# A hybrid mLSTM/GLA layer: the modulation sums beside the GLA branch get GpSimd's queue, more accumulators and more gate buffers

## The chip, the cores and the metric

The kernel runs on one core of one Trainium2 chip. Its engines work in parallel, each through its own instructions in order: PE (matmuls), DVE (VectorE), ACT (ScalarE), POOL (GpSimd) and SP (SyncE, which here only issues DMAs). An instruction that waits holds up everything behind it on its engine. DMAs are issued by SP, ACT or GpSimd, each with a queue of its own, and are carried out by 16 DMA engines. The metric is device time in microseconds of one execution; lower is better. The profiled execution is one among these, and times inside the program are counted from its start.

## What is computed

One layer over 1024 latent tokens with 1024 channels, and 256 context tokens. What matters here, cut from the reference:

```python
mod = jax.nn.silu(c) @ w_mod[l] + b_mod[l]                 # 6 x 1024 values, from a 1024 x 6144 matrix
sh1, sc1, g1, sh2, sc2, g2 = jnp.split(mod[:, None, :], 6, axis=-1)
# ... input projections of h * (1 + sc1) + sh1, two mLSTM scans, two GLA scans ...
y_m = (head_norm(h_m, mlstm_norm_g, True) * jax.nn.sigmoid(o_m)) @ w_branch_mlstm
y_g = (head_norm(h_g, gla_norm_g, False) * jax.nn.silu(z_g)) @ w_branch_gla
mix = (jax.nn.sigmoid(gate_a) * y_m + jax.nn.sigmoid(gate_b) * y_g) @ w_out
h = layer_norm(ALPHA * h + g1 * mix, ln1_g[l], ln1_b[l])
f = conv_glu(h * (1 + sc2) + sh2, rows, *ffn)
h = layer_norm(ALPHA * h + g2 * f, ln2_g[l], ln2_b[l])
```

`sh1` and `sc1` are needed at the start. The other 4096 values of `mod` (`g1`, `sh2`, `sc2`, `g2`) are needed only after the branch stages, and are computed in the middle of the kernel: for this 16.8 MB of `w_mod` have to be read.

## The kernel before

Everything is float32. A matmul is made of three in a faster format: each operand is split into a high part (ACT copies it, `L252`) and a low part (DVE or GpSimd subtracts, `L253`), and `mm3` (`L283` to `L285`) adds high x high, high x low and low x high over eight blocks of 128 channels: 24 matmuls of 128 x 512 for one half of an output tile (512 tokens). `wload` loads a weight matrix 256 columns at a time, in four pieces through four `raw` buffers (`L263`, issued by SP), and splits each into `whi` and `wlo` (six buffers each).

The program runs in stages: modulation and projections, the scans with projections beside them, then four stages which this change touches:

- `gated` for the GLA branch: the projection `z_g` is computed, ACT and DVE make the gated value (`L933` to `L939`), which is split into `hi` (ACT) and `lo` (GpSimd), one tile of 128 channels after the other.
- the GLA branch: eight tiles of 128 output channels, two halves each. For a half, a saved `gate_b` half is loaded into `th` (a tile named `gt`, two buffers; SP, `L954`), ACT takes its tanh (`L955`), PE computes `w_branch_gla` times the gated values into PSUM (tags `pj`, `pa`, `po` in turn, two buffers each), DVE multiplies (`L958`), and SP stores the half to DRAM (`ya`, `L959`).
- `gated` for the mLSTM branch, and the mLSTM branch, built the same way (`th` again, `L994` to `L999`).

Beside tile j of the GLA branch the j-th of eight sums of the modulation is made. `mod_sum(j)` takes an accumulator (`acc`, in slot `u17` or `u19` in turn), GpSimd clears it (`L901`), SP loads 512 values of `b_mod` into its first row (`L903`), and four tiles of `w_mod` of 128 x 2 x 512, 512 KB each, come through two buffers in the slots `u16` and `u18` (`L906`, SP). DVE adds each tile with two instructions (`L908`), each multiplying by a column of silu(c). `mod_row(j)` adds the accumulator's 128 partitions with a matmul by ones on PE (`L913`, two matmuls in the profile), DVE copies the result back (`L914`), SP writes it to `md_d` in DRAM (`L915`). Row j - 1 follows tile j. All these slots are also used by the `gated` stages for other data.

The order in which each engine carries out its instructions is fixed when the program is built, by a scheduler that moves instructions ahead where it expects room. So SP's queue mixes loads of weights, of `w_mod`, of gate halves and stores of results, and one that waits holds up the rest. A tile's buffer is used again only when all that read or wrote it has ended; loading from DRAM into it has to wait for that.

Of the kernel before, what the change touches and what calls it, by code (L numbers as in the profile page):

```python
# [6 lines left out]
F32 = mybir.dt.float32  # L7
# [4 lines left out]
ALU = mybir.AluOpType  # L12
# [3 lines left out]
P = 128  # L16
# [20 lines left out]
def layer_kernel(ctx, tc, I, out, dbg=None):  # L37
    nc = tc.nc
    V, A, G, T, SY = nc.vector, nc.scalar, nc.gpsimd, nc.tensor, nc.sync
    I = {n: (a[0] if n not in ("x", "c", "ctx", "c_ctx") else a) for n, a in I.items()}  # L40
# [13 lines left out]
    def nm(s):  # L54
        cnt[0] += 1
        return f"{s}_{cnt[0]}"

    def pt(tag, shape):
        return ps.tile(shape, F32, tag=tag, name=nm(tag))
# [4 lines left out]
    def slot(i, shape, dt=F32):  # L64

        if i in (8, 9, 10, 11) and sl is sl0:
            n = 1
            for w in shape[1:]:
                n *= w
            tag = "kk" if i < 10 else "qq"  # L70
            if i % 2 == 0:
                half[tag] = sl.tile([P, 2, n], dt, tag=tag, name=nm(tag))
            v = half[tag][0:shape[0], i % 2, :]
            return v if len(shape) == 2 else v.rearrange("p (a b) -> p a b", b=shape[2])
        return sl.tile(shape, dt, tag=f"s{i}", name=nm(f"s{i}"))

    def ubt(i, shape, dt=F32):
        return ub.tile(shape, dt, tag=f"u{i}", name=nm(f"u{i}"))

    def drt(name, shape, dt=F32):  # L80
        return dr.tile(shape, dt, tag=name, name=name)
# [6 lines left out]
    scn = ExitStack()  # L88
    sc = scn.enter_context(tc.tile_pool(name="scn", bufs=1))
# [3 lines left out]
    ones = cst.tile([P, 1], F32, name="ones")  # L93
# [59 lines left out]
    sC = cst.tile([P, KD, 2], F32, name="sC")  # L153
# [19 lines left out]
    raw = slot(7, [P, KD, 64])  # L173
# [20 lines left out]
    for k in range(KD):  # L194
        for b in range(3):
            T.matmul(mps[b][0:2, :], sC[:, k, :], wm[2 * k + b // 2][:, b % 2 * 512:b % 2 * 512 + 512],
                     start=k == 0, stop=k == KD - 1)
# [30 lines left out]
    def cB(i):  # L228
        return colB[:, i:i + 1]
# [21 lines left out]
    def split(hi, lo, src, eng=G):  # L251
        A.activation(hi, src, AF.Copy)  # L252
        eng.tensor_tensor(lo, src, hi.bitcast(F32), op=ALU.subtract)  # L253
# [25 lines left out]
    def mm3(p, lhs, rhs, nk=KD):  # L279
        for k in range(nk):  # L280
            lh, ll = lhs(k)
            rh, rl = rhs(k)
            T.matmul(p, lh, rh, start=k == 0, stop=False)  # L283
            T.matmul(p, lh, rl, start=False, stop=False)  # L284
            T.matmul(p, ll, rh, start=False, stop=k == nk - 1)  # L285
# [37 lines left out]
    def proj(w, c, b, tag="pj"):  # L323
        p = pt(tag, [P, 512])
        mm3(p[:, 0:BW[b]], lambda k: w(k, c, P), u_blk(b))
        return p
# [68 lines left out]
    p = proj(w0, P, 2)  # L395
# [144 lines left out]
    def gla_qk(h):  # L540
        w = wload([(w_in, O_QG + h * P, P, 0), (w_in, O_KG + h * P, P, P)], eng=V)
        q = slot(0, [P, SEQ])
        k = slot(1, [P, L])
        for b in range(2):
            p = proj(w, 0, b)
            A.activation(q[:, b * 512:b * 512 + 512], p[:], AF.Identity, scale=QS, bias=cB(c_qg + h))
        for b in range(3):
            p = proj(w, P, b)
            A.activation(k[:, b * 512:b * 512 + BW[b]], p[:, 0:BW[b]], AF.Identity, bias=cB(c_kg + h))
        return q, k  # L550
# [311 lines left out]
    for h in range(GH):  # L862
        q, k = gla_qk(h) if h else (q0, k0)
# [24 lines left out]


    md_d = drt("md_d", [4096])  # L890

    tags = ("pj", "pa", "po")
    seq = [0]

    def ytag():
        seq[0] += 1
        return tags[seq[0] % 3]

    def mod_sum(b):
        acc = ubt((17, 19)[b % 2], [P, 512])  # L900
        G.memset(acc[:], 0.0)  # L901
        c0 = 2048 + b * 512
        SY.dma_start(acc[0:1, :], I["b_mod"][c0:c0 + 512].unsqueeze(0))  # L903
        for k2 in range(0, KD, 2):
            raw = ubt((16, 18)[k2 // 2 % 2], [P, 2, 512])
            SY.dma_start(raw[:], I["w_mod"][k2 * P:(k2 + 2) * P, c0:c0 + 512].rearrange("(k p) c -> p k c", p=P))  # L906
            for i in range(2):
                V.scalar_tensor_tensor(acc[:], raw[:, i, :], sC[:, k2 + i, 0:1], acc[:], op0=ALU.mult, op1=ALU.add)  # L908
        return acc

    def mod_row(b, acc):
        p = pt("pt", [P, 512])
        T.matmul(p[0:1, :], ones[:], acc[:], start=True, stop=True)  # L913
        V.tensor_copy(acc[0:1, :], p[0:1, :])  # L914
        SY.dma_start(md_d[b * 512:b * 512 + 512].unsqueeze(0), acc[0:1, :])  # L915

    def gated(off, cb0, src_d, silu):
        hi, lo = [], []
        for j2 in range(4):
            w = wload([(w_in, off + j2 * 256, 256, 0)])  # L920
            for e in range(2):
                j = 2 * j2 + e
                hi.append(slot(j, [P, SEQ], F32R))
                lo.append(slot(8 + j, [P, SEQ], F32R))
                hr = ubt(16 + j % 2, [P, SEQ])
                SY.dma_start(hr[:], src_d[j][:])
                ht = ubt(18, [P, SEQ])
                zz2 = ubt(19, [P, 2, 512]) if silu else None
                for b in range(2):
                    s_ = slice(b * 512, b * 512 + 512)  # L930
                    p = proj(w, e * P, b, ytag())
                    th = sc.tile([P, 512], F32, tag="gt", name=nm("gt"), bufs=2)
                    A.activation(th[:], p[:], AF.Tanh, scale=0.5, bias=cB(cb0 + j))  # L933
                    hs = hr[:, s_]
                    if silu:
                        zt = zz2[:, b, :]
                        A.activation(zt, p[:], AF.Identity, scale=0.5, bias=cB(cb0 + j))
                        V.tensor_tensor(hs, zt, hs, op=ALU.mult)
                    V.scalar_tensor_tensor(ht[:, s_], th[:], 1.0, hs, op0=ALU.add, op1=ALU.mult)  # L939
                    split(hi[j][:, s_], lo[j][:, s_], ht[:, s_])  # L940
        return hi, lo
# [3 lines left out]
    accs = {}  # L945
    for j2 in range(4):
        w = wload([(I["w_branch_gla"], j2 * 256, 256, 0)])
        for e in range(2):
            j = 2 * j2 + e
            accs[j] = mod_sum(j)  # L950
            for b in range(2):
                s_ = slice(b * 512, b * 512 + 512)
                th = sc.tile([P, 512], F32, tag="gt", name=nm("gt"), bufs=2)
                SY.dma_start(th[:], thb_d[j][:, s_])  # L954
                A.activation(th[:], th[:], AF.Tanh)  # L955
                p = pt(ytag(), [P, 512])
                mm3(p[:], lambda k: w(k, e * P, P), lambda k: (ghi_[k][:, s_], glo_[k][:, s_]))
                V.scalar_tensor_tensor(th[:], th[:], 1.0, p[:], op0=ALU.add, op1=ALU.mult)  # L958
                SY.dma_start(ya_d[j][:, s_], th[:])  # L959
            if j:  # L960
                mod_row(j - 1, accs[j - 1])
    mod_row(7, accs[7])

    rowF = ubt(19, [P, 3, P])
# [19 lines left out]
    for j2 in range(4):  # L984
        w = wload([(I["w_branch_mlstm"], j2 * 256, 256, 0)])
        for e in range(2):
            j = 2 * j2 + e
            ya = ubt(16 + j % 2, [P, SEQ])
            SY.dma_start(ya[:], ya_d[j][:])
            xhi.append(ubt(j, [P, SEQ], F32R))  # L990
            xlo.append(ubt(8 + j, [P, SEQ], F32R))
            for b in range(2):
                s_ = slice(b * 512, b * 512 + 512)
                th = sc.tile([P, 512], F32, tag="gt", name=nm("gt"), bufs=2)  # L994
                SY.dma_start(th[:], tha_d[j][:, s_])
                A.activation(th[:], th[:], AF.Tanh)
                p = pt(ytag(), [P, 512])
                mm3(p[:], lambda k: w(k, e * P, P), lambda k: (mhi_[k][:, s_], mlo_[k][:, s_]))
                V.scalar_tensor_tensor(th[:], th[:], 1.0, p[:], op0=ALU.add, op1=ALU.mult)  # L999
                V.tensor_tensor(ya[:, s_], th[:], ya[:, s_], op=ALU.add)  # L1000
                split(xhi[j][:, s_], xlo[j][:, s_], ya[:, s_])
    scn.close()
    slx.close()
    sl = ctx.enter_context(tc.tile_pool(name="sl2", bufs=1))

# [102 lines left out]
    for f in range(NF):  # L1108
# [7 lines left out]
        for b in range(2):  # L1116
            for e, (dst, bi) in enumerate(((gf, f), (val, NF + f))):
                p = pt("pj", [P, 512])
# [16 lines left out]
        acc = fp.tile([P, ROWS, GRID_W], F32, tag="acc", name=nm("acc"), bufs=2)  # L1135
        A.activation(acc[:], g, AF.Identity, scale=convw(4, f), bias=cb[:, f:f + 1])  # L1136
        for ky in range(3):
            for kx in range(3):
                if ky == 1 and kx == 1:
# [3 lines left out]
                c0, c1 = max(0, -dx), GRID_W - max(0, dx)  # L1143
                av = acc[:, r0:r1, c0:c1]
                V.scalar_tensor_tensor(av, g[:, r0 + dy:r1 + dy, c0 + dx:c1 + dx], convw(3 * ky + kx, f), av,  # L1145
                                       op0=ALU.mult, op1=ALU.add)
# [20 lines left out]
    gt, yt = {}, {}  # L1167
# [46 lines left out]
    for i, (g, cb_, k) in enumerate(main):  # L1214
        k0, k1 = ((0, N_RES), (N_RES, NF))[g]
        s_ = slice(cb_ * 512, cb_ * 512 + 512)
        if k == k0:
            acc = [pt(b, [P, 512]) for b in bt]
# [42 lines left out]
    for t in range(8):  # L1261
        for cb_ in (1,):
            p = pt(("pj", "pa", "po", "pt")[t % 4], [P, 512])
# [34 lines left out]
```

## Time and profile before

| | |
|---|---|
| median of 3 runs | 2292.91 us (2291.26 to 2295.82) |
| time of the profiled execution | 2294.39 us, span 2292.6 us |
| PE busy | 2235.5 us, 98% of the span |
| DVE busy | 1321.3 us, 58% |
| DMA, mean | 108 GB/s |
| GLA branch stage and around, 1180 to 1290 us | PE busy 102.83 of 110 us, DMA share 0.81, 255 GB/s |
| w_mod loads of 512 KB in all | 48, of these 32 in this stage |

Views of the profile are named in the text. In a stretch, the columns are the length, the busy time of PE, PE's weight loads, DVE, ACT and POOL (with the number of instructions), the granted PE clock as a share of full speed, the busy share of the DMA engines and GB/s. A view of waits names who waited for what, with the total in us, the number of times and the longest. The timeline has the start, the length, the engine, line and operation, and in brackets the idle time before it and what ended it. The chain of waits has start, length and what the time went to. Tile names appear without their numbers: `u` is any of the slots `u0` to `u19`, `s` any of the slots of the scans.

### The profile page before, as it was taken

The numbers are of one execution on the slowest core, as the hardware profiler recorded it, in microseconds if no ns is written. First come the engines' busy times: TensorE is split into PE (matmuls) and PEld (weight loads), VectorE is DVE, ScalarE is ACT, GpSimd is POOL, SyncE is SP. The second block draws the span as 40 slices with busy tenths as digits, with TensorE's granted clock in tenths as the row PEclk, the third lists the DMA queues.
The fourth block names the chain that finished last, engine by engine and source line by source line (L and its number), as shares of the span: only waits on it lengthen the run. The fifth ranks groups of instructions, "written<-read, shape, count | busy, mean of one in ns | idle before, by whom it ended". The sixth has DMA issues, their size and how long they took to land. (4 is left out here: it accounts for less than half of the span.)

```text
span 2292.6 us, 30337 instructions
## 1 busy us (share of the span) xinstructions
PE 2235.5 (98%) x11641; PEld 1881.5 (82%) x11641; DVE 1321.3 (58%) x2511; ACT 728.8 (32%) x1239; POOL 253.3 (11%) x254
## 2 busy tenths in 40 slices
PE   8989999998999999998999899999999999999998
PEld 4979898987889889897887688787888888888886
DVE  6485737376663665755356523578855656654257
ACT  3563323234233332312431233313333333333110
POOL 1010101021110111101210122102111000000000
PEclk9999999999999999999999999999999999999999
DMA  8231221204332433323358634514311222225731
GB/s 287 69 118 52 60 70 39 67 27 107 88 103 66 119 97 102 101 80 110 96 158 264 206 102 148 192 65 163 113 46 46 65 69 78 74 104 176 216 83 74
DMA packets 187746, 246.55 MB, mean 108 GB/s; under 512 B 16257, under 2 KB 129537, under 8 KB 187601
## 3 DMA queue, kind: packets, MB, share of 16 engines
q1 hardware_dynamic: 164673, 179.16, 25.1%
q0 software_dynamic: 12416, 44.21, 7.3%
q10 hardware_dynamic: 10512, 21.24, 2.5%
q8 instruction: 91, 1.49, 0.3%
q14 instruction: 54, 0.44, 0.1%
HBM read 186.57 MB, written 49.60 MB: 103 GB/s over the span
## 5 line engine op out<-in xcount | busy, mean ns | idle before, releaser
L253 DVE TENSOR_TENSOR wlo<-raw,whi 128x512 fp32r<-128x512 f32 x302 | 216.2, 721 | 166.8 <-ACT whi L252 162.0
L283 PE MATMUL pj<-s,whi 128*128 128x512 f32 x784 | 305.6, 390 | 0.3 <-ACT val L1121 0.3
L285 PE MATMUL pj<-s,wlo 128*128 128x512 f32 x784 | 305.4, 390 | 0.0
L252 ACT ACTIVATE whi<-raw 128x512 fp32r<-128x512 f32 x302 | 188.5, 629 | 337.7 <-PE pj L285 151.8
L284 PE MATMUL pj<-s,whi 128*128 128x512 f32 x744 | 290.4, 390 | 3.0 <-POOL s L1089 2.9
L1145 DVE SCALAR_TENSOR_TENSOR acc<-g,colF,acc 128x945 f32<-128x945 f32 (+2 forms) x168 | 206.4, 1229 | 139.6 <-ACT acc L1136 137.5
L283 PE MATMUL pj<-u,whi 128*128 128x512 f32 (+1 forms) x528 | 207.1, 392 | 4.8 <-ACT whi L252 4.8
L285 PE MATMUL pj<-u,wlo 128*128 128x512 f32 (+1 forms) x528 | 206.2, 391 | 0.0
L284 PE MATMUL pj<-u,whi 128*128 128x512 f32 (+1 forms) x528 | 205.9, 390 | 0.0
L283 PE MATMUL pj<-whi,u 128*128 128x256 f32 x640 | 181.5, 284 | 0.0
L285 PE MATMUL pj<-whi,u 128*128 128x256 f32 x640 | 181.4, 283 | 0.0
L284 PE MATMUL pj<-wlo,u 128*128 128x256 f32 x640 | 181.4, 283 | 0.0
L283 PEld LDWEIGHTS pj<-s,whi 128*128 128x128 f32 x784 | 147.2, 188 | 33.3 <-issue 1.7
L285 PEld LDWEIGHTS pj<-s,wlo 128*128 128x128 f32 x784 | 147.2, 188 | 30.9
L284 PEld LDWEIGHTS pj<-s,whi 128*128 128x128 f32 x744 | 139.7, 188 | 34.3 <-POOL s L1089 4.2
L283 PE MATMUL pa<-u,whi 128*128 128x512 f32 (+1 forms) x376 | 142.1, 378 | 2.2 <-DVE s L727 2.2
L284 PE MATMUL pa<-u,whi 128*128 128x512 f32 (+1 forms) x376 | 141.9, 377 | 0.0
L285 PE MATMUL pa<-u,wlo 128*128 128x512 f32 (+1 forms) x376 | 141.2, 376 | 0.0
L284 PEld LDWEIGHTS pj<-wlo,u 128*128 128x128 f32 x640 | 122.8, 192 | 0.0
L283 PEld LDWEIGHTS pj<-whi,u 128*128 128x128 f32 x640 | 122.8, 192 | 0.1
L285 PEld LDWEIGHTS pj<-whi,u 128*128 128x128 f32 x640 | 122.8, 192 | 0.0
L283 PEld LDWEIGHTS pj<-u,whi 128*128 128x128 f32 x528 | 100.2, 190 | 24.1 <-ACT whi L252 5.2
(500 smaller groups left out, 4361.9 us busy)
## 6 DMA issues: line engine op xcount, KB each, us to landing
u<-in_w_mod_dram SPq DMA_DIRECT2D x48, 512.0 KB
raw<-in_w_in_dram SPq DMA_DIRECT2D x96, 256.0 KB
raw<-in_w_up_dram SPq DMA_DIRECT2D x176, 128.0 KB
raw<-in_w_in_dram SPq DMA_DIRECT2D x96, 128.0 KB
raw<-in_w_down_dram SPq DMA_DIRECT2D x44, 256.0 KB
s<-rmask POOLq DMA_DIRECT2D x16, 512.0 KB, 4.7
s<-rr POOLq DMA_DIRECT2D x16, 512.0 KB, 8.7
qq<-re POOLq DMA_DIRECT2D x16, 512.0 KB, 6.6
```

The costliest lines, as they stand in the source:

```text
L252: A.activation(hi, src, AF.Copy)
L253: eng.tensor_tensor(lo, src, hi.bitcast(F32), op=ALU.subtract)
L283: T.matmul(p, lh, rh, start=k == 0, stop=False)
L284: T.matmul(p, lh, rl, start=False, stop=False)
L285: T.matmul(p, ll, rh, start=False, stop=k == nk - 1)
L1145: V.scalar_tensor_tensor(av, g[:, r0 + dy:r1 + dy, c0 + dx:c1 + dx], convw(3 * ky + kx, f), av, op0=ALU.mult, op1=ALU.add)
```

## The change

`scn`, the pool of the scans' small tiles, is closed before the branch stages, and a new pool in its room holds the gate halves, six buffers where there were two. The `w_mod` tiles are issued by GpSimd and no longer by SP. An accumulator is now a half of a pair, two sums in one slot, so that four are there. Row j - 2 follows tile j, and rows 6 and 7 follow the stage.

```diff
+    scn.close()
+    scn2 = ExitStack()
+    sc2 = scn2.enter_context(tc.tile_pool(name="scn2", bufs=1))
...
+    pair = []
+
     def mod_sum(b):
-        acc = ubt((17, 19)[b % 2], [P, 512])
-        G.memset(acc[:], 0.0)
+        if b % 2 == 0:
+            pair.append(ubt((17, 19)[b // 2 % 2], [P, 2, 512]))
+        acc = pair[-1][:, b % 2, :]
+        G.memset(acc, 0.0)
         c0 = 2048 + b * 512
         SY.dma_start(acc[0:1, :], I["b_mod"][c0:c0 + 512].unsqueeze(0))
         for k2 in range(0, KD, 2):
             raw = ubt((16, 18)[k2 // 2 % 2], [P, 2, 512])
-            SY.dma_start(raw[:], I["w_mod"][k2 * P:(k2 + 2) * P, c0:c0 + 512].rearrange("(k p) c -> p k c", p=P))
+            G.dma_start(raw[:], I["w_mod"][k2 * P:(k2 + 2) * P, c0:c0 + 512].rearrange("(k p) c -> p k c", p=P))
             for i in range(2):
-                V.scalar_tensor_tensor(acc[:], raw[:, i, :], sC[:, k2 + i, 0:1], acc[:], op0=ALU.mult, op1=ALU.add)
+                V.scalar_tensor_tensor(acc, raw[:, i, :], sC[:, k2 + i, 0:1], acc, op0=ALU.mult, op1=ALU.add)
         return acc
...
-                    th = sc.tile([P, 512], F32, tag="gt", name=nm("gt"), bufs=2)
+                    th = sc2.tile([P, 512], F32, tag="gt", name=nm("gt"), bufs=6)
...
-            if j:
-                mod_row(j - 1, accs[j - 1])
+            if j > 1:
+                mod_row(j - 2, accs[j - 2])
+    mod_row(6, accs[6])
     mod_row(7, accs[7])
...
-    scn.close()
+    scn2.close()
```

The line of `th` changes in both `gated` stages and both branch stages.

How this moves instructions shows best at two places. The first is PE's queue at the end of the GLA branch. The first row here is the end of tile 7 (`po`), then come rows of the modulation (`pt`, with `ones`) and the first half tile of the next stage (`pj`, three matmuls for each of the eight blocks), then the second (`pa`). Before:

```order
L285 MATMUL po_11173<-s_1474_10378,wlo_11035 128x512
L913 MATMUL pt_11200<-u_1590_11038,ones 1x512
L283 MATMUL pj_11261<-u_46_299,whi_11234 128x512
...
L285 MATMUL pj_11261<-u_51_304,wlo_11247 128x512
L283 MATMUL pa_11291<-u_46_299,whi_11234 128x512
...
L284 MATMUL pa_11291<-u_56_309,whi_11240 128x512
L913 MATMUL pt_11204<-u_1600_11121,ones 1x512
L285 MATMUL pa_11291<-u_48_301,wlo_11241 128x512
```

And with the change:

```order
L285 MATMUL po_11169<-s_1474_10382,wlo_11032 128x512
L920 MATMUL pt_11196<-u_1555_10846,ones 1x512
L920 MATMUL pt_11200<-u_1586_11035,ones 1x512
L283 MATMUL pj_11261<-u_46_299,whi_11234 128x512
...
L284 MATMUL pj_11261<-u_59_312,whi_11246 128x512
L920 MATMUL pt_11204<-u_1586_11035,ones 1x512
L285 MATMUL pj_11261<-u_51_304,wlo_11247 128x512
```

Before, row 6 follows tile 7 and row 7 stands behind 26 matmuls of the next stage (18 of `pj`, 8 of `pa`). Now rows 5 and 6 follow tile 7 together, and row 7 stands behind 17 matmuls, in the middle of the first half tile.

The second place is the queue that issues `w_mod`. On SP before, at tiles 6 and 7 (`thb` is the gate half, `ya` the stored result, `md_d` the row, `raw` a piece of the next stage's weights):

```order
L906 DMA u_1594_11053<-in_w_mod_dram 128x2x512
L959 DMA ya_9792<-gt_11087 128x512
L915 DMA md_d<-u_1568_10931 1x512
L954 DMA gt_11140<-thb_873 128x512
L906 DMA u_1601_11124<-in_w_mod_dram 128x2x512
L903 DMA u_1600_11121<-in_b_mod_dram 1x512
L906 DMA u_1602_11128<-in_w_mod_dram 128x2x512
L959 DMA ya_9793<-gt_11140 128x512
L954 DMA gt_11170<-thb_873 128x512
L263 DMA raw_11244<-in_w_in_dram 128x2x256
```

On GpSimd with the change, from the last split of the first `gated` stage to the pair of tiles 4 and 5 (`u_1555`):

```order
L253 TENSOR_TENSOR s_1475_10383<-u_1477_10386,s_1474_10382 128x512
L913 DMA u_1497_10483<-in_w_mod_dram 128x2x512
L913 DMA u_1498_10487<-in_w_mod_dram 128x2x512
...
L913 DMA u_1537_10754<-in_w_mod_dram 128x2x512
L913 DMA u_1556_10849<-in_w_mod_dram 128x2x512
L908 MEMSET u_1555_10846 128x512
L913 DMA u_1557_10853<-in_w_mod_dram 128x2x512
L908 MEMSET u_1555_10846 128x512
L913 DMA u_1558_10857<-in_w_mod_dram 128x2x512
```

The `w_mod` loads have left SP, and stand one behind the other on GpSimd; the only other instructions among them are the memsets of the pairs, each in front of a load. The four memsets of the first two pairs, and the first load, stand ahead of the split at the top.

More of the change, by code (lines that the diff above doesn't have):

```diff
@@ L912, in mod_row @@
         p = pt("pt", [P, 512])
-        T.matmul(p[0:1, :], ones[:], acc[:], start=True, stop=True)
+        T.matmul(p[0:1, :], ones[:], acc, start=True, stop=True)
         V.tensor_copy(acc[0:1, :], p[0:1, :])
@@ L952, in layer_kernel @@
                 s_ = slice(b * 512, b * 512 + 512)
-                th = sc.tile([P, 512], F32, tag="gt", name=nm("gt"), bufs=2)
+                th = sc2.tile([P, 512], F32, tag="gt", name=nm("gt"), bufs=6)
                 SY.dma_start(th[:], thb_d[j][:, s_])
@@ L993, in layer_kernel @@
                 s_ = slice(b * 512, b * 512 + 512)
-                th = sc.tile([P, 512], F32, tag="gt", name=nm("gt"), bufs=2)
+                th = sc2.tile([P, 512], F32, tag="gt", name=nm("gt"), bufs=6)
                 SY.dma_start(th[:], tha_d[j][:, s_])
```

## The prediction

> **What bounds the kernel now.** I read the page's engine shares first, then the stage that the diff touches in stretches of 20 us, then the waits of PE and DVE there, then the chain of waits inside it.
>
> ```profile
> PE 2235.5 (98%) x11641; PEld 1881.5 (82%) x11641; DVE 1321.3 (58%) x2511; ACT 728.8 (32%) x1239; POOL 253.3 (11%) x254
> ```
> ```profile
> 1160.00:1180.00 20.00, 20.00 (x90) 16.52 (x89) 8.54 (x12) 9.20 (x15) 4.82 (x5) 1.00 0.29 92
> ...
> 1260.00:1280.00 20.00, 18.65 (x74) 12.80 (x73) 12.80 (x18) 2.52 (x4) 1.05 (x2) 1.00 0.78 250
> 1280.00:1300.00 20.00, 15.54 (x59) 11.61 (x60) 11.23 (x16) 5.58 (x9) 2.62 (x2) 0.91 0.66 206
> ```
>
> PE sets the time nearly everywhere: 90 matmuls in 20 us just before the stage. In the GLA branch stage, to whose second half the other two stretches belong, it falls to 74 and 59, while the DMA engines are busiest (0.66 to 0.78, against 0.29). What PE waits for there, and what DVE waits for:
>
> ```profile
> PE pj L283 <- ACT whi L252: 4.8, 1, 4.8
> PE pt L913 <- DVE u L908: 2.4, 3, 1.4
> ```
> ```profile
> DVE u L908 <- DMA u<-in_w_mod_dram: 23.6, 20, 2.7
> DVE u L908 <- DMA u<-in_b_mod_dram: 5.2, 2, 3.3
> DVE gt L958 <- ACT gt L955: 4.1, 5, 1.9
> ```
>
> PE loses 7.2 us: 2.4 at the modulation rows, 4.8 at the next stage's first weights. That is all that waits can give back here, plus a slow clock behind the long wait (below). The chain of waits says why:
>
> ```profile
> 1229.54 4.87 DMA u<-in_w_mod_dram
> 1234.50 0.76 DVE u L908
> 1235.28 0.76 DVE u L908
> 1236.06 5.70 DMA u<-in_w_mod_dram
> ...
> 1243.77 4.49 DMA u<-in_w_mod_dram
> ...
> 1249.92 4.36 DMA u<-in_w_mod_dram
> ...
> 1255.94 4.88 DMA u<-in_w_mod_dram
> ...
> 1262.48 5.71 DMA u<-in_w_mod_dram
> ...
> 1271.78 5.07 DMA gt<-thb
> ...
> 1279.15 4.53 DMA raw<-in_w_in_dram
> ...
> 1284.46 0.80 PE pj L283
> ```
>
> Until 1268 one buffer of two sets the pace: load it (mean of the first five 4.86 us), sum it (2 x 0.76), and only then load it again. One round is (1262.48 - 1229.54) / 5 = 6.6 us, two tiles of w_mod pass in it, and there are 32: about 16 rounds. SP is never late in it: the next load leaves 0.02 us behind the sum (1235.28 + 0.76 to 1236.06). Later the chain runs over a gate half (gt) and the weights queued behind it on SP. **So the stage has two limits close together: the round trip of w_mod, and SP's order.**
>
> **The change part by part.**
>
> *Six gate-half buffers.* They take away DVE's 4.1 us behind L955 and let SP issue w_in (L263) before 1279.15, so the 4.8 us at the first weights lose their cause. In the second branch stage, where the same buffers serve, DVE waits for PE and not for gates, so I count nothing there:
>
> ```profile
> DVE gt L999 <- PE pj L285: 17.5, 5, 4.2
> ```
>
> *Loads on GpSimd's queue.* The round keeps its two buffers (u16, u18); only its transfer changes. The trace has no w_mod load on that queue. The nearest rows are its other 512 KB loads from DRAM:
>
> ```profile
> gl<-gl POOLq DMA_DIRECT2D x12, 512.0 KB, 4.6
> u<-n POOLq DMA_DIRECT2D x8, 512.0 KB, 4.0
> ```
> ```profile
> 2070.67 1.23 DVE L253 TENSOR_TENSOR s<-gl,s 128x1024 fp32r<-128x1024 f32 x1 [3.61 <-ACT s L252]
> 2072.19 0.53 POOL L1171 DMA_DIRECT2D gl<-gl  x1 [4.91 <-DVE s L253]
> 2076.12 1.06 ACT L252 ACTIVATE s<-gl 128x1024 fp32r<-128x1024 f32 x1 [2.83 <-DMA gl<-gl]
> ```
>
> GpSimd starts 0.29 us after DVE lets the buffer go (2071.90 to 2072.19); SP needed 0.02. From there it takes 4.0 (u<-n) to 4.6 us (gl). The DMA engines of the branch stage are 0.66 to 0.78 busy, so I take the longer row: 0.29 + 4.6 = 4.9, against 4.88 now. **The round stays at 6.6 us; this term is 0.** Its ends: with 4.0 a round of 6.0, -0.6 x 15.5 = -9 us (of 16 rounds the first is half under way); with 5.2 (about halfway to 5.71, the slowest of the chain above, and 4.6) 7.2, +9 us.
>
> *What is queued on GpSimd.* Four memsets now stand ahead of the last split of the gated stage, where two stood, and the second w_mod load waits for that split:
>
> ```profile
> 1179.46 0.53 POOL L901 MEMSET u<- 128x512 f32 x1 [2.48 <-DVE u L938]
> ...
> 1180.88 1.29 POOL L253 TENSOR_TENSOR s<-u,s 128x512 fp32r<-128x512 f32 x1 [0.16 <-ACT s L252]
> 1206.60 0.53 POOL L901 MEMSET u<- 128x512 f32 x1 [24.43 <-DMA md_d<-u]
> ```
>
> Two more of 0.53 make the split up to 1.1 later, or 0 if all four fit into the 2.48 before it; the pair in u17 is let go just before, by DVE, so I take the upper part: **+0.8.** For tiles 4 and 6 the memset waits for an earlier row to reach DRAM, and a w_mod load stands behind it. Row, copy, store and memset end about when the buffer of that load comes free; I count 0.4 us each, bounds 0 and 1.5. **+0.8.** PE's matmuls do not wait for GpSimd meanwhile; its next split follows in the next gated stage.
>
> *Four accumulators.* They end some waits of DVE for b_mod. Bounds: 0, and 5.2 + 4.1 with the gates. Most of these ran beside a w_mod load in flight, which would have been awaited next: the longest one began its sum at 1211.54 where the load had left at 1205.60, and 4.86 later is 1210.5, so 1.1 of 3.28 was lost. The five gate waits were mostly short; of the 9.3 I take a fifth. **-2.0 for both.**
>
> ```profile
> 1205.60 0.38 SPq L906 DMA_DIRECT2D u<-in_w_mod_dram  x1
> ```
> ```profile
> 1211.54 1.54 DVE L908 SCALAR_TENSOR_TENSOR u<-u,sC,u 128x512 f32<-128x512 f32 x2 [3.28 <-DMA u<-in_b_mod_dram]
> ...
> 1286.83 1.54 DVE L908 SCALAR_TENSOR_TENSOR u<-u,sC,u 128x512 f32<-128x512 f32 x2
> ```
>
> The last sum, now done at 1288.4, ends at 1288.4 + 0 + 0.8 + 0.8 - 2.0 = **1288.0**.
>
> *Rows two tiles later.* For rows 0 to 5 this gives the 2.4 us back. The last rows have no two tiles left, and PE's order decides: row 7 came after 26 matmuls of the next stage, and now comes after 17.
>
> ```profile
> 1274.48 0.40 PE L285 MATMUL po<-s,wlo 128*128 128x512 f32 x1
> ...
> 1284.46 0.80 PE L283 MATMUL pj<-u,whi 128*128 128x512 f32 x1 [4.80 <-ACT whi L252]
> ```
> ```profile
> 1286.97 0.43 PE pj L285
> ...
> 1288.14 0.23 PE pa L285
> ...
> 1289.50 0.95 PE pt L913 x2
> ```
> ```profile
> 1286.00:1288.00 2.00, 2.00 (x7) 1.58 (x6) 1.81 (x3) 0.00 (x0) 0.00 (x0) 0.53 0.93 194
> ```
>
> PE's last branch matmul ended near 1274.7; without 2.4 of waits and with one row (0.95) less ahead, 1271.4. Two rows and 17 matmuls at 0.23 bring it to row 7 at 1277.2, where it stands until the last sum, 1288.0. **So the wait moves: rows 6 and 7 now hold some 10 us, where 7.2 were lost.** Behind row 7 are 9 more matmuls than before (9 x 0.23 = 2.0). After the 4.80 us wait the granted clock was 0.53 and eight matmuls took 0.43 instead of 0.23; before, this fell ahead of row 7 and was hidden, now it comes behind: 8 x 0.2 = 1.6. Sum: (1288.0 + 0.1) - 1289.5 + 2.0 + 1.6 = **+2.2 us**. The profiled execution (span 2292.6, time 2294.39) lies 1.5 above the median 2292.91; the difference is put on the median: **2295 us**.
>
> **The rivals.**
>
> *The round gets faster.* For it: on its own queue a w_mod load no longer stands behind gates and stores; u<-n landed in 4.0. Against it: gl took 4.6, and the load of 1262.48, which took 5.71, left 1.8 us behind another w_mod load (1260.64, below), which own queues do not part. With a round of 6.0 the last sum ends near 1279, PE stands 2 us and the clock holds: 1279.1 - 1289.5 + 2.0 = -8.4, **2285**. It cannot gain much more, since PE is not at row 7 before 1277.2. The Trainium skill (DMA: Bandwidth & Descriptors, section Queues, rings and completion order) says that each DMA engine takes turns between queues by packets; that speaks for this rival, and no run here shows it yet.
>
> *The round gets slower, and PE stands longer at row 7.* The shortest load of the stage on SP took 4.00; GpSimd's above took 3.93 + 0.29 = 4.22:
>
> ```profile
> 1260.64 0.38 SPq L906 DMA_DIRECT2D u<-in_w_mod_dram  x1
> ```
> ```profile
> 1264.64 1.54 DVE L908 SCALAR_TENSOR_TENSOR u<-u,sC,u 128x512 f32<-128x512 f32 x2 [1.14 <-DMA u<-in_w_mod_dram]
> ```
>
> With 0.2 more per round under the same crowding, 15.5 x 0.2 = 3.1 more: +5.4, **2298**; with a landing of 5.2, +11, 2304. It decides from a round of 6.75 us on. Against it: SP's traffic is spread better by six buffers. The Trainium skill (same page, section Specifications) gives about 1 us to the first byte for a DMA from GpSimd and 0.6 for one from SP; an estimate by it adds 0.4 to each round beside the 0.29, some 10 us, and 2305. The two rows just quoted, 3.93 and 4.00 from the start, do not show that 0.4.
>
> *The change does not do what it says:* the waits it removes had cover, as w_mod set the pace anyway. That is inside the forecast.
>
> **How the numbers follow.** Round unchanged within 0.15: 0.42, 2295, own range 2289 to 2298. Faster round: 0.25, 2285. Slower: 0.33, 2298 to 2304. A measurement of this kernel tells about 0.2%, 4.6 us, from no change: faster 0.25, same 0.42, slower 0.33. The range 2285 to 2304 takes in landings from 4.0 to 5.2.
>
> **What would show it.** Right: w_mod still ahead of the sums in the chain of waits, rounds near 6.6, PE's waits at rows 6 and 7 near 10 us in all, none left at the first weights, w_in issued before 1270, the last sum near 1288. Wrong: a round under 6.3 or over 6.8, or a row 7 that does not wait.

## The result

The changed kernel takes 2312.95 us (median of 6 runs, 2307.61 to 2315.54), the kernel before 2293.04 us (6 runs on the same chip, 2291.26 to 2295.82). The ratio is 1.0083, with a 95% interval of 1.0072 to 1.0093: **slower by about 20 us**, above the predicted range of 2285 to 2304. It went the way of the second rival, and further.

Where the 21.0 us between the two profiled spans (2292.6 and 2313.6) arise is read from marks in the two timelines. The last split of the gated stage is the first mark:

```profile
1183.20 0.63 ACT L252 ACTIVATE s<-u 128x512 fp32r<-128x512 f32 x1 [1.49 <-DVE u L946]
```

In the kernel before the same instruction starts at 1180.16. Of the change, the gate buffers, the clearing of the first accumulators and the first `w_mod` load stand ahead of it; but in the kernels below except e10, most of which have these too, it starts anywhere from 1177.51 (e7) to 1183.73 (e4), with six gate buffers as with two. So I take 3.0 of the 21.0 us as chance between two executions. From here on "the end" means the time from this mark to the end of the span: 1112.4 us before, 1130.4 now, **+18.0**. This is what I compare, beside the medians.

PE's waits in the branch stage, and the stretches that answer to those shown of before:

```profile
PE pt L920 <- DVE u L915: 12.2, 2, 11.2
PE po L283 <- ACT whi L252: 3.0, 1, 3.0
PE pa L285 <- DVE wlo L253: 2.2, 1, 2.2
PE pa L283 <- ACT whi L252: 1.1, 1, 1.1
PE po L285 <- DVE wlo L253: 0.3, 1, 0.3
```
```profile
1260.00:1280.00 20.00, 16.70 (x56) 11.82 (x56) 12.46 (x19) 2.71 (x5) 5.21 (x8) 0.83 0.75 232
1280.00:1300.00 20.00, 13.62 (x54) 9.08 (x52) 13.37 (x20) 2.53 (x4) 3.79 (x6) 0.93 0.67 190
1300.00:1320.00 20.00, 14.20 (x50) 10.12 (x51) 5.42 (x10) 2.64 (x4) 2.49 (x2) 0.73 0.39 130
```

PE stands 18.8 us where it stood 7.2, most of it (11.2) at one place, row 7. The four waits for weights are at the branch's own pieces, in tiles 4 and 6; the next stage's weights are awaited no more. The DMA engines move less than before, not more (232 and 190 GB/s where it was 250 and 206). DVE's waits name what is late:

```profile
DVE u L915 <- DMA u<-in_w_mod_dram: 41.2, 23, 3.2
DVE u L915 <- DMA u<-in_b_mod_dram: 3.0, 2, 2.1
```

41.2 us for w_mod, where it was 23.6. The chain of waits inside the stage, its last part:

```profile
1267.80 6.21 DMA u<-in_w_mod_dram
1274.10 0.76 DVE u L915
1274.89 0.76 DVE u L915
1275.65 0.29 issue
1275.94 4.99 DMA u<-in_w_mod_dram
...
1282.57 0.29 issue
1282.86 4.95 DMA u<-in_w_mod_dram
...
1289.75 4.86 DMA u<-in_w_mod_dram
1294.65 2.35 issue
1297.01 6.62 DMA u<-in_w_mod_dram
...
1305.08 0.67 DVE u L915
1305.80 1.86 PE pt L920 x2
1307.66 0.73 PE pj L285
1308.39 0.43 PE pj L283
```

One buffer's round trip is now the whole stage, up to row 7. Each round has a piece that it did not have before, 0.29 us in which GpSimd gets going, and several of the loads take 6 us and more. (The 2.35 us of "issue" ahead of the last load are the two sums that empty its buffer, begun at 1294.70, and the 0.29 behind them: the view names another releaser.) Behind row 7 the matmuls take 0.43 us in place of 0.23: the granted clock is down to 0.73 in that stretch.

**How the 18.0 come together.** The sums of the second load and of the last one:

```profile
1191.33 1.54 DVE L915 SCALAR_TENSOR_TENSOR u<-u,sC,u 128x512 f32<-128x512 f32 x2 [2.44 <-DMA u<-in_w_mod_dram]
...
1305.00 0.75 DVE L915 SCALAR_TENSOR_TENSOR u<-u,sC,u 128x512 f32<-128x512 f32 x1
```
```profile
1186.79 1.54 DVE L908 SCALAR_TENSOR_TENSOR u<-u,sC,u 128x512 f32<-128x512 f32 x2 [1.89 <-DMA u<-in_w_mod_dram]
```

The first fence is the timeline of the changed kernel, the second of the kernel before, whose last sum (shown with the prediction) ended at 1288.37. Fifteen rounds lie between: 112.9 us now (7.53 each), 100.0 before (6.67), +12.8. The second load's sums end 9.7 us behind the mark instead of 8.2, +1.5. So the last sum is 14.3 us later. PE now stands right at it (row 7 starts 0.05 behind the sum, before 1.13): -1.1. Nine more matmuls come behind row 7: +2.1. Seven of them at 0.43 instead of 0.23: +1.4. Row 7 itself takes 1.86 instead of 0.95: +0.9. Together 17.6 of 18.0.

### The profile page after: what moved, and what is told of

It is laid out like the page before. It is cut to its first block, busy times and chain, and to the rows that moved or that the text cites. A ratio compares the mean times of both kernels' runs of the same rounds, so it can differ in the third digit from the quotient of the medians.

```text
span 2313.6 us, 30321 instructions
## 1 busy us (share of the span) xinstructions
PE 2242.8 (97%) x11641; PEld 1884.9 (81%) x11641; DVE 1318.7 (57%) x2511; ACT 728.3 (31%) x1239; POOL 276.3 (12%) x286
## 4 chain that ended last, share of the span: by engine, by line
PE 83%; DMA 7%; DVE 5%; issue 3%; ACT 1%; POOL 0%; SPq 0%; DVEq 0%; POOLq 0%; ACTq 0%
PE pj L285 15%; PE pj L284 15%; PE pj L283 15%; DMA u<-in_w_mod_dram 5%; PE pa L283 4%; PE pa L284 4%; PE pa L285 4%; PE pa L618 2%; PE pt L796 1%; PE po L816 1%; PE po L817 1%; PE po L283 1%; PE po L284 1%; PE po L285 1%; PE pt L659 1%
## 5 line engine op out<-in xcount | busy, mean ns | idle before, releaser
L283 PEld LDWEIGHTS pj<-whi,u 128*128 128x128 f32 x640 | 122.6, 192 | 0.1
L284 PEld LDWEIGHTS pj<-wlo,u 128*128 128x128 f32 x640 | 122.7, 192 | 0.0
L285 PEld LDWEIGHTS pj<-whi,u 128*128 128x128 f32 x640 | 122.6, 192 | 0.0
L285 PEld LDWEIGHTS pj<-u,wlo 128*128 128x128 f32 x528 | 100.4, 190 | 19.3 <-issue 1.7
```

## The experiments

Theory 1: the way through GpSimd lengthens the round. Theory 2: the six gate buffers crowd the w_mod loads out. Theory 3: the new places of the rows make PE stand. For each kernel three means over the loads 3 to 32 of the stage are worked out from the timeline: from a buffer's release (the end of its second sum) to the next load's start; from the start to the first sum; and the length of the two sums. Their sum is the round. The time from the start to the first sum holds the landing, and also whatever else DVE waits for before the sum.

| kernel | queue of w_mod | release to start | start to first sum | two sums | round | last sum behind the mark | the end, against before | median us (ratio, interval) |
|---|---|---|---|---|---|---|---|---|
| before | SP | 0.09 | 5.05 | 1.59 | 6.73 | 108.2 | 0 | 2293.04 |
| changed | GpSimd | 0.34 | 5.43 | 1.70 | 7.48 | 122.6 | +18.0 | 2312.95 (1.0072 to 1.0093) |
| e1 loads on SP | SP | 0.04 | 4.83 | 1.64 | 6.50 | 105.9 | -0.1 | 2295.03 (0.9999 to 1.0017) |
| e2 queue only | GpSimd | 0.34 | 5.58 | 1.74 | 7.66 | 122.7 | +17.3 | 2309.62 (1.0057 to 1.0087) |
| e3 third buffer | GpSimd | | | | | 110.6 | +12.2 | 2307.37 (1.0047 to 1.0081) |
| e4 rows one tile later | GpSimd | 0.34 | 5.37 | 1.80 | 7.51 | 122.0 | +17.0 | 2312.42 (1.0071 to 1.0101) |
| e5 no gates | GpSimd | 0.34 | 4.68 | 1.70 | 6.72 | 109.5 | +4.4 | 2300.25, one run |
| e6 no gates | SP | 0.03 | 4.57 | 1.74 | 6.34 | 102.6 | -2.5 | 2291.79, one run |
| e7 wide rows | GpSimd | 0.33 | 5.46 | 1.70 | 7.49 | 121.3 | +18.2 | 2311.25 (1.0076 to 1.0109) |
| e8 four buffers | GpSimd | | | | | 104.1 | +7.6 | 2301.12 (1.0028 to 1.0058) |
| e9 on ACT | ACT | 0.07 | 5.27 | 1.67 | 7.01 | 114.9 | +9.5 | 2302.74, one run |
| e11 before, on ACT | ACT | 0.13 | 5.56 | 1.65 | 7.35 | 118.3 | +14.1 | 2309.03, one run |
| e12 as e4, on ACT | ACT | 0.18 | 4.92 | 1.72 | 6.82 | 111.1 | +8.9 | 2304.37, one run |
| e10 sums earlier | SP | | | | | | | 2289.36 (0.9974 to 0.9994) |

With more than two buffers (e3, e8) and in e10 a load no longer follows the second load before it, so no round is given. The ends, and every mean here, come from one profiled execution of each kernel.

### e1 and e2: the queue undone, and the queue alone

```diff
-            G.dma_start(raw[:], I["w_mod"][...])
+            SY.dma_start(raw[:], I["w_mod"][...])     # e1: the changed kernel; e2 is the reverse, in the kernel before
```

> The changed kernel with one thing undone: the w_mod loads go through SP's queue again; six gate buffers, four accumulators and late rows stay. Theory 1 (the way through GpSimd lengthens each round of a w_mod buffer, from 6.6 to 7.4 us, and that delays the last sum): the round goes back to about 6.6 us, the last sum ends some 13 us sooner, row 7 waits 1 to 3 us instead of 11.2, and the time is 2293 to 2299. Theory 2 (six gate buffers let gate halves and stores go sooner, and their traffic crowds the w_mod tiles out): the round stays above 7.2 us and the time is 2308 or more. Theory 3 (the new places of the rows make PE stand): the last sum is sooner, but the time stays within 4 us of 2313.

> The kernel before with one thing changed: the w_mod loads are issued by GpSimd; two gate buffers, two accumulators and rows one tile later stay. Theory 1 (the way through GpSimd): the round grows to about 7.4 us, the last sum ends 12 to 15 us later, PE waits 8 to 14 us at row 7 or at the next weights, time 2303 to 2312. Theory 2 (six gate buffers crowd the DMA engines): no change from before, 2290 to 2296. Theory 3 (rows): no change either, since the rows stand as before.

The two answer each other. Without the queue, all the rest of the change gives 2295.03, where the kernel before took 2293.27 in the same series; with nothing but the queue, 2309.62. Theories 2 and 3 fall: six gate buffers and late rows are in e1, and cost nothing that can be measured. The chain of waits of e1, its longest pieces:

```profile
1205.59 4.80 DMA u<-in_w_mod_dram
1211.98 4.29 DMA u<-in_w_mod_dram
1217.92 4.66 DMA u<-in_w_mod_dram
...
1232.49 4.02 DMA raw<-in_w_branch_gla_dram
...
1249.64 4.80 DMA raw<-in_w_branch_gla_dram
...
1280.34 4.10 DMA raw<-in_w_in_dram
```
```profile
PE pj L283 <- ACT whi L252: 5.0, 2, 2.9
PE po L283 <- ACT whi L252: 1.8, 1, 1.8
```

On SP the other edits do shorten the stream of w_mod: its last sum ends 2.3 us sooner than before. But PE then waits 6.8 us for weights, which stand behind w_mod in SP's queue, as it waited 7.2 before, and the end does not move (-0.1). In e2, with two accumulators and rows one tile later, PE waits 19.9 us in all, every bit of it at the rows:

```profile
PE pt L913 <- DVE u L908: 19.9, 6, 7.8
```

### e4: rows one tile later again

```diff
-            if j > 1:
-                mod_row(j - 2, accs[j - 2])
-    mod_row(6, accs[6])
+            if j:
+                mod_row(j - 1, accs[j - 1])
```

> The changed kernel with one thing undone: each row follows the next tile, as before, instead of the one after; row 7 stands behind 18 matmuls of the next stage (17 in the changed kernel, 26 before). Theories 1 and 2: the last sum sets the end, and rows 0 to 5 have nothing to do with it: row 7 waits about as long, 2308 to 2315. Theory 3 (rows two tiles later cost the time): 2300 or less.

2312.42, as the changed kernel. Rows 0 to 5 move PE's waits among themselves (17.6 us at five rows, where it was 12.2 at two), and the last sum sets the end all the same.

### e3 and e8: more buffers for w_mod

```diff
+            # e3: every third tile goes to a buffer of 4 KB in the new pool
+            raw = sc2.tile([P, 2, 512], F32, tag="wm", ...)
```
```diff
-            pair.append(ubt((17, 19)[b // 2 % 2], [P, 2, 512]))
+        acc = sc2.tile([P, 512], F32, tag="acc", ..., bufs=4)[:]      # e8; four gate buffers, not six
-            raw = ubt((16, 18)[k2 // 2 % 2], [P, 2, 512])
+            raw = ubt(16 + k2 // 2, [P, 2, 512])
```

> The changed kernel with a third buffer for the w_mod tiles (4 KB a partition in the new pool; the loads stay on GpSimd's queue). Theory 1 (a round's length counts, because only two tiles are in flight): three tiles are in flight, the eight sums keep up with PE, the last sum ends before 1290, PE does not stand at rows 6 and 7, and the 7.2 us of waits of the kernel before are gone: 2283 to 2289. Theory 2 (the DMA engines are full in this stage): landings grow from 5.0 to 7 us, the last sum hardly moves, 2306 to 2314. Theory 3 (rows): as theory 1 in the sums; the time falls with them by the 11.2 us of the wait at most, 2301 or more.

> Loads on GpSimd's queue, with four w_mod buffers (u16 to u19), four gate buffers, and four accumulators of 2 KB in the new pool that come free one by one (in the run with a third buffer the pairs came free late and the sums stood 15 and 10 us). If a round's length was the limit, it no longer sets the pace: the last sum ends before 1280, row 7 does not wait, 2284 to 2292. If the DMA engines' share is the limit: loads take 8 us or more to land, and 2300 or more.

Both expectations of mine were too good, and for reasons worth seeing. In e3 the sums did run ahead, and then stood for an accumulator. A pair comes free only when both its rows are in DRAM, and row 1 stands on PE behind tile 3. GpSimd's memset waited for that, and the loads behind it:

```profile
1227.11 1.54 DVE L920 SCALAR_TENSOR_TENSOR u<-u,sC,u 128x512 f32<-128x512 f32 x2 [1.84 <-DMA u<-in_w_mod_dram]
1243.54 1.54 DVE L920 SCALAR_TENSOR_TENSOR u<-u,sC,u 128x512 f32<-128x512 f32 x2 [6.79 <-DMA u<-in_b_mod_dram]
```

That is 15 us without one sum. e8, with accumulators that come free one by one, has its last sum 104.1 us behind the mark, sooner than in the kernel before (108.2). So the length of the round is no longer what sets the end there; yet the end is +7.6. The stretches of e8 show one place where PE stands, and the chain of waits what led to it:

```profile
1180.00:1200.00 20.00, 20.00 (x88) 16.16 (x87) 11.34 (x16) 3.17 (x5) 6.91 (x9) 1.00 0.94 326
1200.00:1220.00 20.00, 15.42 (x53) 11.10 (x52) 14.14 (x22) 3.97 (x7) 5.32 (x8) 0.83 0.90 306
```
```profile
1192.80 6.34 DMA ya<-gt
1199.16 4.59 DMA gt<-thb
1203.98 0.41 issue
1204.39 0.62 ACT whi L252
1205.05 0.80 PE pj L283
```
```profile
DVE acc L911 <- DMA acc<-in_b_mod_dram: 22.7, 4, 7.5
```

With four tiles of w_mod in flight the DMA engines are 0.94 busy. PE waits 4.6 us for the high part of the branch's weights, at a place where before there was none, and the clock falls to 0.83. The loads of these weights had left SP by 1179.2; late was ACT, which stood for a gate half, and this one had to wait for a store of 6.34 us to empty its buffer. Later DVE waits 22.7 us for biases, most of which stood in SP's queue behind stores and gate halves, and PE 4.5 us more at a row. So the round's length was one limit, and the next one lies in SP's queue of gate halves, stores and biases. How much of that is the busy DMA engines, and how much that e8 has four gate buffers and not six, no run here separates. Landings of 8 us or more, the sign that I had named for full DMA engines, did not come: the view of DMA issues gives a median of 5.9.

### e5, e6 and e7: what in GpSimd's way costs the time

```diff
-                SY.dma_start(th[:], thb_d[j][:, s_])
-                A.activation(th[:], th[:], AF.Tanh)
+                A.activation(th[:], ones[:].to_broadcast([P, 512]), AF.Tanh)
...
-                SY.dma_start(ya_d[j][:, s_], th[:])
```

> The changed kernel without SP's bulk traffic beside the w_mod loads: in the GLA branch stage the gate halves are not loaded (the tanh takes a constant) and the results are not stored (the second branch reads another tensor), so its output is not the reference's. w_mod stays on GpSimd's queue. Measured is the mean from a load's start on GpSimd to its first sum (5.43 us in the changed kernel, 5.05 on SP before) and the round. Theory A (the way through GpSimd costs the time whatever else moves): 5.2 to 5.5 us, round 7.2 or more. Theory B (on a queue of its own the load shares the DMA engines with SP's traffic, on SP's queue it had them to itself): 4.3 to 4.7 us, round 6.3 to 6.7.

> The control for the run without gate halves and stores: the same work left out, w_mod on SP's queue (with the gates: 4.83 us from start to sum, round 6.50). Theory A: GpSimd's round stays some 0.9 us longer than this one. Theory B: the two differ by 0.3 us at most, which is GpSimd's later start (0.34 against 0.04 us).

With SP's bulk traffic beside them, a load from GpSimd takes 0.60 us longer from start to sum than one from SP (5.43 and 4.83); without it, 0.11 (4.68 and 4.57). But the 4.57 of e6 hold waits that are not the load's, and e5 has none of these:

```profile
DVE u L915 <- DMA u<-in_b_mod_dram: 6.0, 2, 3.2
```

6.0 us of waiting for b_mod over 30 loads is 0.20 us for each. About 4.37 is left in e6, and the difference without the bulk traffic is 0.31. The start stays 0.30 us later in both. The landings that the view of DMA issues gives, of the changed kernel and of e5:

```profile
u<-in_w_mod_dram POOLq DMA_DIRECT2D x31, 512.0 KB, 5.0
```
```profile
u<-in_w_mod_dram POOLq DMA_DIRECT2D x31, 512.0 KB, 4.3
```

The view gives no such figure for SP. But the traces keep the start of every packet on each queue, and the semaphore steps by which a load reports its landing, and these settle the question without DVE. (A first packet is counted only for loads that found their own queue empty. The table gives the range in which most of these lie; the others came later, up to 2.2 us on GpSimd and 1.9 on ACT.)

| from the start of the DMA instruction, us | GpSimd | SP | ACT |
|---|---|---|---|
| to the first packet, 256 rows of 2 KB, most loads | 1.42 to 1.48 | 1.01 to 1.04 | 1.02 to 1.08 |
| to the first packet, 128 rows of 4 KB (e7), most loads | 1.22 to 1.27 | | |
| to the landing, mean, with gate halves and stores | 5.27 (changed), 5.36 (e2), 5.27 (e4), 5.11 (e7) | 4.83 (before), 4.60 (e1) | 5.03 (e9), 4.88 (e11), 4.84 (e12) |
| the same without them | 4.59 (e5) | 4.24 (e6) | |

So of the 0.98 us between the rounds of the changed kernel and e1, 0.30 are GpSimd's late start and about 0.4 its later first packet, and both are there with SP's bulk traffic and without it. The landings without it differ by 0.35, with it by 0.67; two kernels with the loads on SP differ by 0.23 (4.83 and 4.60), so whether the last 0.3 need that traffic is not shown. Theory A held for most of the difference. The traffic lengthens the loads of either queue: that is why e5 met theory B's range for the way from start to sum (4.68), though not for the round (6.72), and the rounds of e5 and e6 differ by 0.38, not by 0.3 at most.

```diff
-            raw[:] <- w_mod[k2 * P:(k2 + 2) * P, c0:c0 + 512]     # 256 rows of 2 KB
+            raw[:] <- w_mod[k * P:(k + 1) * P, c0:c0 + 1024]      # 128 rows of 4 KB, for two sums
```

> The changed kernel with w_mod tiles of the same 512 KB taken as 128 rows of 4 KB (one block of channels for two sums) instead of 256 rows of 2 KB; on GpSimd's queue. Theory A, by pieces (each row costs GpSimd's way something): the DMA instruction falls from 0.72 to 0.53 us as for the gl tiles, start to sum falls by 0.2 to 0.6 us, the round to 6.9 to 7.2, and the time to 2300 to 2308. Theory A, by load (a fixed cost), or B: round 7.3 to 7.6, time 2309 to 2316.

The DMA instruction on GpSimd fell from 0.72 to 0.53 us as expected, and the first packet comes 0.2 us sooner (the table above). The mean landing fell from 5.27 to 5.11 us, less than I expected, and it became no time: 5.46 us from start to sum (two sums waited for the memset, which now clears a whole pair, 3.0 us in all), round 7.49, 2311.25. The rows cost GpSimd's way a little; most of what it costs is there with half as many of them.

### e9, e11 and e12: a third queue

```diff
-            G.dma_start(raw[:], I["w_mod"][...])
+            A.dma_start(raw[:], I["w_mod"][...])      # e9 changed kernel, e11 kernel before (there from SY), e12 = e4
```

> The changed kernel with the w_mod loads on ACT's queue: a queue apart from SP's as GpSimd's is, but issued by another engine. Measured is the mean from a load's start to its first sum (5.43 us from GpSimd, 4.83 from SP, both with the gate halves) and from a buffer's release to the next load's start. Theory B (any queue beside SP's shares the DMA engines with it): 5.2 to 5.6 us. Theory A (GpSimd's own way is what costs): 4.7 to 4.95 us. The start will be late by 0.5 to 3 us in both, since ACT stands for gate halves in its own order, so the time says little: 2300 to 2330.

> The kernel before with its w_mod loads on ACT's queue, nothing else changed: a second look at whether any queue beside SP's costs what GpSimd's does (the first run on ACT's queue gave a mean of 5.27 us from start to sum, between the two; two of its 30 loads, 8.9 us each, waited for an accumulator's bias and not for their data, and without them it is 5.01). If sharing with SP's queue is enough: 5.3 to 5.6 us, as from GpSimd (5.37 to 5.58 in four kernels). If GpSimd's way is needed for it: 4.8 to 5.1 us, as from SP (4.83 and 5.05), and a round of 6.6 to 6.9.

> The kernel with six gate buffers, four accumulators and rows one tile later (5.37 us and a round of 7.51 from GpSimd), with its w_mod loads on ACT's queue. Sharing enough: 5.3 to 5.6 us, round 7.0 or more, 2304 or more. GpSimd's way needed: 4.8 to 5.1 us, round 6.5 to 6.8, 2293 to 2300.

Is any queue beside SP's as slow? e9 fell between the two expectations (5.27). e12, the cleanest of the three since no accumulator waits for its bias in it, gave 4.92 us, SP's side; GpSimd gave 5.37 with the same arrangement (e4). In e11 the 5.56 hold waits that are not the load's:

```profile
DVE u L908 <- DMA u<-in_w_mod_dram: 25.0, 19, 2.7
DVE u L908 <- DMA u<-in_b_mod_dram: 17.4, 6, 5.5
```

17.4 us of waiting for b_mod over 30 loads is 0.58 us for each; about 5.0 is left. So three looks at ACT's queue give 4.9 to 5.0 us, SP's two 4.8 to 5.05, GpSimd's four kernels with traffic 5.4 to 5.6: most of the extra is GpSimd's own. The landings agree: 0.43 us between e4 and e12, 0.48 between e2 and e11, which differ in nothing but GpSimd or ACT, and the first packet alone makes 0.4 of that. Why GpSimd's first packet comes later, no run here shows. ACT's queue is no way out either: ends of +9 to +14, because ACT, too, does its work in order, and gate halves, splits and weights came late behind it. The round of e11 (7.35, expected 6.6 to 6.9) and the time of e12 (2304.37, expected 2293 to 2300) were misses. (For e11 and e12 I compare inside the trace alone: the kernel before took 2299.26 in its one run of that series.)

The Trainium skill (DMA: Bandwidth & Descriptors, section Issuing engines are not separate DMA queues) says that DMAs started from several engines run on the same 16 DMA engines, so that starting them elsewhere saves only the issuing engine's time. The runs agree that nothing is saved, and show a loss beside that: each of the six kernels besides the changed one that did the full work with w_mod on a queue of its own and two buffers for it (e2, e4, e7, e9, e11, e12) has an end between +9 and +18.

### e10: sums where the DMA engines are free

```diff
+    def mod_pieces(n, tags_): ...            # n tiles of 256 KB, each loaded by SP and summed at once
+    gated(..., hg_d, True, 5): mod_pieces(5, None) in each of its eight tiles     # five of the eight sums
+    branch: mod_pieces(4, (16, 17, 18, 19)) in tiles 0 to 5                       # the other three
```

> A version meant to beat both kernels. Five of the eight sums are made beside the eight tiles of the gated stage before the GLA branch (five tiles of 256 KB each), where the DMA engines are only 0.28 to 0.37 busy, the other three beside tiles 0 to 5 of the branch stage; all loads on SP's queue, four gate buffers, two accumulators in the new pool, each row after the tile that follows its sum. If the branch stage's transfers are what costs PE its 7.2 us of waits and the slow clock behind them, these go: 2282 to 2287. Rival: DVE stands for w_mod in its own order and lets PSUM or the gated values come late, so PE stands in the gated stage: 2291 or more.

2289.36 (2285.77 to 2292.59) against 2292.45 in the same series, ratio 0.9984 (0.9974 to 0.9994): faster than both kernels, though by less than expected (2282 to 2287). PE's waits between 1060 and 1420 us:

```profile
PE pa L283 <- ACT whi L252: 0.9, 1, 0.9
PE po L285 <- DVE wlo L253: 0.7, 1, 0.7
PE pj L284 <- DMA u<-in_w_mod_dram: 0.4, 1, 0.4
```
```profile
1100.00:1120.00 20.00, 20.00 (x90) 16.57 (x89) 15.95 (x19) 9.38 (x16) 5.59 (x4) 1.00 0.63 199
...
1280.00:1300.00 20.00, 20.00 (x90) 16.40 (x89) 4.62 (x10) 5.12 (x8) 3.93 (x3) 1.00 0.23 71
```

2.0 us are left of the 7.2, PE does not stand in the gated stage, though DVE is nearly twice as busy there (15.95 us in the stretch, before 8.55), and the clock holds. The waits account for 5.2 us; why the median shows only 3, I have not settled.

## Why the prediction was wrong

**The step that failed is the term "Loads on GpSimd's queue", put at 0.** It took 0.29 us of start and 4.6 us of landing for 4.9 in place of 4.88 on SP. The start was right (0.29 in the chain, 0.34 as a mean with waits). The landing was not: loads from GpSimd in this stage landed after 5.27 us in the mean and took 5.43 from start to sum, up to 7.2. The round grew to 7.5, not 6.6, and fifteen rounds make 12.8 us. The range's own end (a landing of 5.2, a round of 7.2, +9) was too near as well. Two things about the row that the 4.6 came from, gl, I did not weigh. A gl load is 128 rows of 4 KB, and in the kernel before its first packet comes 1.25 us behind the start; a w_mod load is 256 rows of 2 KB, and needs 1.45 from GpSimd where SP needs 1.02. And gl loads run where the DMA engines are 0.60 to 0.75 busy, while the branch stage has 0.81 from end to end (the 0.66 to 0.78 that I read are its second half); e5 shows that GpSimd's landing depends on the company (4.59 to 5.27), as SP's does (4.24 to 4.60).

- *The rival "The round gets slower, and PE stands longer at row 7"* is what happened, in its mechanism and its place. Its point of decision, 6.75, was passed; its price, +11 at most, was short by the size of the round. Its chance of 0.33 was below that of a round unchanged.
- *The Trainium skill's estimate* (the page named there, Specifications: 0.4 us more to the first byte from GpSimd, hence 2305) pointed the right way, and I set it aside because two loads did not show it, one of them a gl load with its shorter way. The traces bear the 0.4 out, as the difference of the first packets (1.42 to 1.48 us behind the start from GpSimd, 1.01 to 1.04 from SP), and with it a round of 7.3 in place of 6.6; the measured one is 7.5.
- *The rival "The round gets faster"*, for which a queue of its own spoke, fell: with its own queue, a load from GpSimd landed later, not sooner (e1, e2).
- *Memsets ahead of the split, +0.8*: the second load starts 2.8 us behind the mark, before 2.0. Right. *Memsets of tiles 4 and 6, +0.8*: no load started late by them. The memset of tile 4 did wait 1.94 us for its row, and the bias behind it made one sum 2.1 us late; but that was in the other buffer's rounds, not in those that ended last. In the sum of the 18.0 this term is nothing.
- *Four accumulators and six gate buffers, -2.0*: e1 holds them without GpSimd, and its last sum is 2.3 us sooner. Right in size. That this becomes no time, because weights then wait (6.8 us in e1), was not foreseen.
- *Rows*: right in mechanism. Row 7 stands behind 17 matmuls, PE waits there (12.2 us at two rows, forecast some 10), the slow clock falls behind it (0.43 us a matmul). Rows two tiles later neither help nor harm (e4).
- *Six gate buffers let w_in go before 1270*: the first pieces left at 1244.98 and 1264.69, and PE waited for no weights of the next stage. But 6.6 us of waits at the branch's own weights, which lay under the later wait at row 7, were not forecast.
- *The sum of all other terms*, +2.2 us, is what e1 took: 2295.03 measured, 2295 predicted. The forecast was that of a kernel whose w_mod loads had stayed on SP. But the agreement is partly luck: in e1 PE waits 6.8 us for weights and not at row 7, as the sum had it, its end is -0.1 and not +2.2, and its median cannot be told from the kernel before.

## What to carry to other kernels

When a stream with few buffers sets the pace, a few tenths of a microsecond in its round trip count as often as there are rounds; ask for the whole loop, release to start to landing to use, before moving its queue, and take the landing from a load of the same shape in a stage as busy as the one it goes to. A queue taken off a crowded engine does not make the transfers cheaper: moving part of the same bytes to a stage where they were idler helped (by 3 us), and other queues and more buffers did not. Before adding buffers, look for the next thing that comes free late (here the accumulators, then gate halves and biases).

## What I had not expected of the hardware

- A 512 KB load from GpSimd had its first packet 1.42 to 1.48 us behind the start of its instruction, one from SP 1.01 to 1.04 and one from ACT 1.02 to 1.08; before that, GpSimd starts 0.30 us behind the release of the buffer, SP and ACT 0.03 at best. Together this is 0.7 us for each round.
- The length of GpSimd's DMA instruction (0.72 us for 256 rows of 2 KB, 0.53 for 128 rows of 4 KB, the same 512 KB) shows in the first packet (1.45 and 1.24), and hardly in the round (7.48 and 7.49).
- Nearly the same code ahead of the stage reached the mark at times 6.2 us apart in single executions (1177.51 to 1183.73), so a difference between two profiled spans of that size says nothing before it is placed.
